# Low parts of the unscaled weights computed on GpSimd instead of VectorE, in a four-layer hybrid decoder

## The chip, the cores and the metric

One core of one Trainium2 chip runs the whole program. The metric is the device time of one execution in microseconds; the median of three runs counts. The engines are named as in the profile: PE is TensorE's matrix unit (PEld its weight load), DVE is VectorE, ACT is ScalarE, POOL is GpSimd, SP is SyncE, which issues most of the DMAs.

## What is computed

The reference is a decoder trunk of four layers over 1024 tokens of width 1024, batch 1, all in float32. Layers 0 and 3 mix tokens with an HGRN2 gated linear recurrence (8 heads), layer 1 with sliding-window attention (16 query heads, 4 key/value heads, window 128), layer 2 with a gated DeltaNet (8 query/key heads, 16 value heads, a short causal convolution ahead of it). Cut to the frame:

```python
for i in range(DEPTH):
    mod = (c @ ada_w[i] + ada_b[i])[:, None, :]
    shift, scale, gate = jnp.split(mod, 3, axis=-1)
    h = rmsnorm(x, norm_g[i]) * (1.0 + scale) + shift
    y = mixer[i % 3](h, ...)       # (o * silu(z)) @ w_out, with q, k, v, z from h @ w_in
    x = x + gate * y
return x
```

Most of the arithmetic is in `h @ w_in` and `... @ w_out`.

## The kernel before

**Numbers in two parts.** A projection is not multiplied in plain float32. Weights and activations are split into a high part (type `F32R` in the code) and a low part, the rest: `hi = cast(x)`, `lo = x - hi`. A product is then three matmuls, high by high, and each high by the other's low; `mm3` (L196 to L198) issues them. In the profile these are the groups `proj_ps` (feature-major, 128x512), `projt_ps` (token-major, 128x256) and `outp_ps` (output projection).

**A weight tile's way.** `load_w` (L158 to L178) brings 128x512 floats into a buffer `w_raw` (L169, an SP DMA of 256 KB; tag "raw", three buffers, shared with the modulation weights `ada_w`), makes `w_hi` on ACT and then `w_lo`. There are four buffers each of w_hi and w_lo. So w_raw comes free when w_lo has been made, and w_hi and w_lo when PE has used them. There are two forms. Without a scale (all input projections, and the window layer's output projection) w_hi is an ACT cast (L171) and w_lo a subtraction (L172), 332 of each. With a scale (the other output projections, which fold a norm's gain into the weights) it is L174 and L175, 136 of each.

**What else the engines do.** PE runs the projections and the small matmuls of the mixers. DVE has the elementwise work of the mixers, the normalisations (n_t at L479, then hlo at L481, which reads n_t and hhi), the modulation sums (L403, L405), the convolution taps (L617, L619) and, in the DeltaNet layer, a serial elimination on 32x32 blocks (L750, L751). GpSimd has little: copies of diagonal blocks in the HGRN layers (L1044, `hg_at`), in the DeltaNet layer the convolution's three-column halo (L614, L608), memsets (L606, L741 to L743) and copies of block inverses (L773, L774, L783).

**What sets the order.** The program is written as generators (`weave`) which interleave the recurrence of one head with the projections of the next. A planner then lists the instructions of each engine by priority and by the time at which it reckons each to be ready, so an instruction that changes its engine changes the lists of all engines. On the chip every engine works through its own list in order and waits at semaphores.

**Stages in the profiled execution.** Start to about 60 us; HGRN layer 0 to 580 (its output projection runs on beyond that); changeover into the window layer to 700, window layer to about 1130; changeover into the DeltaNet layer to 1300, its loop over head pairs to 1960, output projection to 2200; HGRN layer 3 to the end.

Of the kernel before, what the change touches and what calls it, by code (L numbers as in the profile page):

```python
# [10 lines left out]
F32 = mybir.dt.float32  # L11
# [5 lines left out]
ALU = mybir.AluOpType  # L17
# [67 lines left out]
class Trunk:  # L85
# [72 lines left out]
    def load_w(self, src, scale=None):  # L158

        nc = self.nc  # L160
        shape = list(src.shape)
        raw = self.wp.tile([P, HT], F32, name="w_raw", tag="raw", bufs=RAW)
        hi = self.wp.tile([P, HT], F32R, name="w_hi", tag="whi", bufs=WB)
        lo = self.wp.tile([P, HT], F32R, name="w_lo", tag="wlo", bufs=WB)
        raw, hi, lo = (x[:, :math.prod(shape[1:])] for x in (raw, hi, lo))
        if len(shape) == 3:
            raw, hi, lo = (x.rearrange("p (a b) -> p a b", a=shape[1]) for x in (raw, hi, lo))
        with self.tc.high_priority(offset=self.pw):
            nc.sync.dma_start(raw, src)  # L169
            if scale is None:  # L170
                nc.scalar.copy(hi, raw)  # L171
                nc.vector.tensor_tensor(lo, raw, hi.bitcast(F32), ALU.subtract)  # L172
            else:
                nc.scalar.activation(hi, raw, AF.Copy, scale=scale)  # L174
                nc.vector.scalar_tensor_tensor(lo, raw, scale, hi.bitcast(F32), ALU.mult, ALU.subtract)  # L175
            n = self.tc.cur_priority
        self.tc.cur_priority = n + self.pw
        return hi, lo  # L178
# [1269 lines left out]
```

## Time and profile before

| | |
|---|---|
| median of three runs | 2753.58 us (2751.43 to 2759.05) |
| the profiled execution | 2752.67 us, span 2751.0 us |
| PE busy | 2669.9 us (97%) |
| DVE busy | 2001.3 us (73%) |
| ACT busy | 1224.1 us (44%) |
| GpSimd busy | 133.8 us (5%) |
| L172 (w_lo without scale) | 332 instructions, 223.1 us on DVE |

A row of a group gives line, engine, operation, output and inputs, shapes and count, then busy time and mean length of one, then the idle time of the engine just ahead of the group and what ended most of it. A row of waits reads "who, line <- for whom, line: us in total, times, longest". A row by stage gives the stretch, its length and then, engine by engine, the busy time and the number of instructions; the last three figures are the granted clock of PE, the busy share of the DMA engines and their GB/s. Rows of the timeline and of the chain begin with the start and the duration in us.

### The profile page before, as it was taken

How to read it: one execution, taken by the hardware profiler on the slowest of the kernel's cores; microseconds unless marked ns; L12 is line 12 of the kernel's file. 1: busy time of each engine (PE TensorE's matmuls, PEld its weight loads, DVE VectorE, ACT ScalarE, POOL GpSimd, SP SyncE). 2: the span in 40 equal slices, each digit the busy share in tenths (PEclk: the TensorE clock that was granted, in tenths of full speed). 3: DMA queues.
4: the chain of work that ended last, by engine and by line, in shares of the span. 5: the costliest groups of instructions: out<-in, count | busy, mean ns of one | idle time of the engine just before them, and what ended most of it. 6: DMA issues, size and time to landing. Idle time of an engine off the chain costs nothing.

```text
span 2751.0 us, 51716 instructions
## 1 busy us (share of the span) xinstructions
PE 2669.9 (97%) x19217; PEld 2147.2 (78%) x19217; DVE 2001.3 (73%) x5669; ACT 1224.1 (44%) x3107; POOL 133.8 (5%) x352
## 2 busy tenths in 40 slices
PE   8999999998999999899999999999999999999999
PEld 4878888778878767677788877787778888887877
DVE  6685765778677778677898798988875757556575
ACT  4332333444445565444546455555543433333342
POOL 0000100000000000001101001100000000000000
PEclk9999999999999999999999999999999999999999
DMA  6232222344223243324343343432463211111133
GB/s 237 82 103 82 66 85 74 118 129 146 62 85 97 77 149 91 116 74 111 94 127 101 92 123 101 116 104 77 150 188 119 81 54 40 51 46 49 46 120 112
DMA packets 347666, 273.30 MB, mean 99 GB/s; under 512 B 68963, under 2 KB 276246, under 8 KB 347414
## 3 DMA queue, kind: packets, MB, share of 16 engines
q1 hardware_dynamic: 347126, 268.95, 32.8%
q8 instruction: 151, 2.47, 0.4%
q14 instruction: 101, 0.83, 0.1%
q0 software_dynamic: 288, 1.05, 0.1%
HBM read 224.77 MB, written 45.15 MB: 98 GB/s over the span
## 4 chain that ended last, share of the span: by engine, by line
PE 76%; DVE 11%; DMA 6%; ACT 4%; issue 2%; SPq 1%; POOL 0%; DVEq 0%; ACTq 0%
PE proj_ps L196 10%; PE proj_ps L198 10%; PE proj_ps L197 10%; PE outp_ps L198 4%; PE outp_ps L196 4%; PE outp_ps L197 4%; PE projt_ps L197 3%; PE projt_ps L198 3%; PE projt_ps L196 3%; DMA ada_w<-in_ada_w_dram 2%; PE lev_ps L1004 2%; DVE gd_tb L617 1%; PE pv_ps L1330 1%; DVE w_lo L172 1%; PE w_ps L859 1%
## 5 line engine op out<-in xcount | busy, mean ns | idle before, releaser
L196 PE MATMUL proj_ps<-hhi,w_hi 128*128 128x512 f32 x1664 | 686.1, 412 | 11.2 <-ACT gd_tb L615 8.6
L197 PE MATMUL proj_ps<-hlo,w_hi 128*128 128x512 f32 x1664 | 675.5, 406 | 0.0
L198 PE MATMUL proj_ps<-hhi,w_lo 128*128 128x512 f32 x1664 | 674.0, 405 | 0.0
L196 PEld LDWEIGHTS proj_ps<-hhi,w_hi 128*128 128x128 f32 x1664 | 315.5, 190 | 68.3 <-ACT gd_tb L615 11.0
L198 PEld LDWEIGHTS proj_ps<-hhi,w_lo 128*128 128x128 f32 x1664 | 314.9, 189 | 59.1 <-issue 1.2
L197 PEld LDWEIGHTS proj_ps<-hlo,w_hi 128*128 128x128 f32 x1664 | 315.3, 190 | 53.0 <-issue 1.4
L172 DVE TENSOR_TENSOR w_lo<-w_raw,w_hi 128x512 fp32r<-128x512 f32 x332 | 223.1, 675 | 168.2 <-ACT w_hi L171 165.6
L171 ACT CAST w_hi<-w_raw 128x512 fp32r<-128x512 f32 x332 | 201.9, 611 | 307.8 <-PE proj_ps L197 183.1
L197 PE MATMUL projt_ps<-w_lo,hhi 128*128 128x256 f32 x896 | 256.1, 290 | 5.8 <-DVE w_lo L172 5.8
L196 PE MATMUL projt_ps<-w_hi,hhi 128*128 128x256 f32 x896 | 256.1, 291 | 0.5 <-ACT w_hi L171 0.5
L198 PE MATMUL projt_ps<-w_hi,hlo 128*128 128x256 f32 x896 | 255.4, 290 | 0.0
L196 PE MATMUL outp_ps<-o_hi,w_hi 128*128 128x512 f32 x576 | 229.3, 400 | 2.9 <-ACT o_hi L1156 1.9
L198 PE MATMUL outp_ps<-o_hi,w_lo 128*128 128x512 f32 x576 | 228.0, 398 | 1.4 <-DVE w_lo L175 1.4
L197 PE MATMUL outp_ps<-o_lo,w_hi 128*128 128x512 f32 x576 | 228.8, 398 | 0.2
L197 PEld LDWEIGHTS projt_ps<-w_lo,hhi 128*128 128x128 f32 x896 | 170.7, 192 | 9.2 <-DVE w_lo L172 6.8
L196 PEld LDWEIGHTS projt_ps<-w_hi,hhi 128*128 128x128 f32 x896 | 170.5, 192 | 3.8 <-issue 1.2
L198 PEld LDWEIGHTS projt_ps<-w_hi,hlo 128*128 128x128 f32 x896 | 170.6, 192 | 2.3 <-issue 1.4
L617 DVE SCALAR_TENSOR_TENSOR gd_tb<-gd_xs,taps,gd_tb 128x512 f32<-128x512 f32 x192 | 144.2, 751 | 25.1 <-ACT gd_tb L615 21.5
L174 ACT ACTIVATE w_hi<-w_raw,par 128x512 fp32r<-128x512 f32 (+1 forms) x136 | 94.7, 698 | 142.9 <-PE outp_ps L197 98.8
L196 PEld LDWEIGHTS outp_ps<-o_hi,w_hi 128*128 128x128 f32 x576 | 108.6, 189 | 27.0 <-ACT o_hi L1156 3.9
L175 DVE SCALAR_TENSOR_TENSOR w_lo<-w_raw,par,w_hi 128x512 fp32r<-128x512 f32 (+1 forms) x136 | 96.8, 716 | 42.8 <-ACT w_hi L174 41.5
L198 PEld LDWEIGHTS outp_ps<-o_hi,w_lo 128*128 128x128 f32 x576 | 108.6, 189 | 24.2 <-DVE w_lo L175 1.9
(388 smaller groups left out, 4918.5 us busy)
## 6 DMA issues: line engine op xcount, KB each, us to landing
ada_w<-in_ada_w_dram SPq DMA_DIRECT2D x160, 256.0 KB, 2.8
w_raw<-in_hg_in_w_dram SPq DMA_DIRECT2D x136, 256.0 KB, 2.8
w_raw<-in_gd_in_w_dram SPq DMA_DIRECT2D x108, 256.0 KB, 3.1
o_in<-od SPq DMA_DIRECT2D x72, 256.0 KB, 3.3
w_raw<-in_gd_out_w_dram SPq DMA_DIRECT2D x64, 256.0 KB, 2.8
w_raw<-in_sw_in_w_dram SPq DMA_DIRECT2D x48, 256.0 KB, 3.0
w_raw<-in_hg_out_w_dram SPq DMA_DIRECT2D x40, 256.0 KB, 2.9
ada_w<-in_ada_w_dram SPq DMA_DIRECT2D x8, 1024.0 KB, 10.0
```

The costliest lines, as they stand in the source:

```text
L171: nc.scalar.copy(hi, raw)
L172: nc.vector.tensor_tensor(lo, raw, hi.bitcast(F32), ALU.subtract)
L174: nc.scalar.activation(hi, raw, AF.Copy, scale=scale)
L175: nc.vector.scalar_tensor_tensor(lo, raw, scale, hi.bitcast(F32), ALU.mult, ALU.subtract)
L196: mm(out, a[0], b[0], start=start, stop=False)
L197: mm(out, a[0], b[1], start=False, stop=False)
L198: mm(out, a[1], b[0], start=False, stop=stop)
L617: nc.vector.scalar_tensor_tensor(y, xs[:, j:j + HT], w(j), y, ALU.mult, ALU.add)
L859: nc.tensor.matmul(po[:, hd[a]], dd["u"][a, hf][:, cs], rhs, start=True, stop=True)
L1004: nc.tensor.matmul(pl[gs, c * 48:(c + 1) * 48], kg[:, c * P + g * 32:c * P + (g + 1) * 32], x[:, 4 * c + g, :], start=True, stop=True)
L1330: nc.tensor.matmul(po[a * 64:(a + 1) * 64], vg[:, n + 1 - nkb + b, :], p4[:, :, a, :], start=b == 0, stop=b == nkb - 1)
```

## The change

One line: where a weight tile has no scale, the subtraction that makes w_lo is issued on GpSimd.

```diff
             if scale is None:
                 nc.scalar.copy(hi, raw)
-                nc.vector.tensor_tensor(lo, raw, hi.bitcast(F32), ALU.subtract)
+                nc.gpsimd.tensor_tensor(lo, raw, hi.bitcast(F32), ALU.subtract)
```

The scaled form (L175) stays on VectorE, and so does every other low part. All 332 move, and the planner's order moves with them on every engine.

On VectorE, at the start of the DeltaNet layer, in the normalisation of the second half of the tokens (x_11272 is that half of x), the order of before has w_lo between the steps:

```order
L466 TENSOR_TENSOR n_sq<-ident,rs_y 128x512
L479 SCALAR_TENSOR_TENSOR n_t<-x_11272,gcol,n_rb 128x512 x2
L481 SCALAR_TENSOR_TENSOR hlo<-n_t,mod,hhi 128x512
L172 TENSOR_TENSOR w_lo<-w_raw,w_hi 128x512
L481 SCALAR_TENSOR_TENSOR hlo<-n_t,mod,hhi 128x512
L172 TENSOR_TENSOR w_lo<-w_raw,w_hi 128x512
L479 SCALAR_TENSOR_TENSOR n_t<-x_11272,gcol,n_rb 128x512 x2
L481 SCALAR_TENSOR_TENSOR hlo<-n_t,mod,hhi 128x512
```

The same place in the changed program, on the same engine:

```order
L466 TENSOR_TENSOR n_sq<-ident,rs_y 128x512
L479 SCALAR_TENSOR_TENSOR n_t<-x_11272,gcol,n_rb 128x512 x2
L481 SCALAR_TENSOR_TENSOR hlo<-n_t,mod,hhi 128x512 x2
L479 SCALAR_TENSOR_TENSOR n_t<-x_11272,gcol,n_rb 128x512 x2
L481 SCALAR_TENSOR_TENSOR hlo<-n_t,mod,hhi 128x512
L479 SCALAR_TENSOR_TENSOR n_t<-x_11272,gcol,n_rb 128x512
```

The five w_lo that stood among these sixteen steps (two are among the rows shown) have left VectorE's list.

On GpSimd, in the DeltaNet loop, where the first block inverse is put together (gd_Tb is the elimination's result of the next head pair, gd_Z and gd_uq hold the assembled inverse, gd_xs and gd_halo belong to the convolution), the order of before:

```order
L741 MEMSET gd_Tb 128x512
L742 MEMSET gd_Tb 64x16
L743 MEMSET gd_Tb 64x16
L773 COPY gd_Z<-gd_Tc 32x16x32
L774 COPY gd_Z<-gd_Tc 32x16x32
L783 COPY gd_uq<-gd_Uc 32x16x32 x4
L614 COPY gd_halo<-gd_xs 128x3
L608 COPY gd_xs<-gd_halo 128x3
```

And in the changed program:

```order
L741 MEMSET gd_Tb 128x512
L172 TENSOR_TENSOR w_lo<-w_raw,w_hi 128x512
L742 MEMSET gd_Tb 64x16
L743 MEMSET gd_Tb 64x16
L172 TENSOR_TENSOR w_lo<-w_raw,w_hi 128x512
L773 COPY gd_Z<-gd_Tc 32x16x32
L774 COPY gd_Z<-gd_Tc 32x16x32
L783 COPY gd_uq<-gd_Uc 32x16x32 x4
L172 TENSOR_TENSOR w_lo<-w_raw,w_hi 128x512 x6
L614 COPY gd_halo<-gd_xs 128x3
L608 COPY gd_xs<-gd_halo 128x3
```

Eight w_lo now stand among the copies, two ahead of those of the block inverse and six between them and the next halo.

## The prediction

> **What bounds the kernel now.** I read the page's busy table first, then the costliest groups, the busy time by stage, the waits, and last the timeline at the places where TensorE (PE) stood still.
>
> ```profile
> span 2751.0 us, 51716 instructions
> PE 2669.9 (97%) x19217; PEld 2147.2 (78%) x19217; DVE 2001.3 (73%) x5669; ACT 1224.1 (44%) x3107; POOL 133.8 (5%) x352
> ...
> L172 DVE TENSOR_TENSOR w_lo<-w_raw,w_hi 128x512 fp32r<-128x512 f32 x332 | 223.1, 675 | 168.2 <-ACT w_hi L171 165.6
> L171 ACT CAST w_hi<-w_raw 128x512 fp32r<-128x512 f32 x332 | 201.9, 611 | 307.8 <-PE proj_ps L197 183.1
> ```
>
> PE is busy for 2669.9 of 2751.0 us. The change takes no matmul away, so all it can win is part of the other 81 us and of short pauses that this busy figure hides. VectorE (DVE) works 73% of the time; GpSimd (POOL) is nearly free.
>
> By stage (columns: PE, PEld, DVE, ACT, POOL busy; PEclk is the granted clock), and below it the part of L172 alone in DVE's time:
>
> ```profile
> 60.00:580.00 520.00, 514.40 (x4550) 424.82 (x4550) 355.80 (x1082) 185.41 (x426) 31.37 (x65) 1.00 0.30 90
> 580.00:700.00 120.00, 108.12 (x672) 93.52 (x672) 94.87 (x220) 50.54 (x95) 1.58 (x4) 0.97 0.42 131
> 700.00:1000.00 300.00, 292.27 (x1951) 234.26 (x1949) 212.14 (x642) 149.16 (x389) 0.00 (x0) 1.00 0.29 90
> 1130.00:1300.00 170.00, 152.30 (x895) 117.51 (x895) 120.73 (x306) 79.05 (x220) 12.97 (x33) 0.96 0.34 91
> 1300.00:1960.00 660.00, 649.42 (x4542) 525.55 (x4541) 571.44 (x1673) 356.02 (x1110) 54.41 (x135) 0.99 0.39 107
> ```
>
> ```profile
> 60.00:580.00 520.00, 44.04 (x64) 1.00 0.30 90
> 1300.00:1960.00 660.00, 52.09 (x76) 0.99 0.39 107
> ```
>
> The long stages (HGRN 60 to 580, the DeltaNet loop 1300 to 1960) leave PE idle for 5.6 and 10.6 us. The changeovers into the window layer (580 to 700) and into the DeltaNet layer (1130 to 1300) leave 11.9 and 17.7 us, and there the granted clock dips as well. In the DeltaNet loop DVE is at 87%.
>
> **The change part by part.**
>
> *What leaves DVE.* 332 instructions of 675 ns. Back to back, a DVE instruction occupies less than its length:
>
> ```profile
> 1243.05 0.69 DVE L172 TENSOR_TENSOR w_lo<-w_raw,w_hi 128x512 fp32r<-128x512 f32 x1
> 1243.65 0.28 DVE L751 TENSOR_TENSOR gd_Tb<-gd_Tb,gd_tmp 128x126 f32<-128x126 f32 x1
> ```
>
> The next one starts 0.60 us later, so 332 x 0.60 = 199 us of DVE's queue go. With them go 165.6 us in which DVE's queue stood still until ACT had made w_hi. Most of both lies beside PE work. What shows on the path is in three waits of PE and the places behind them:
>
> ```profile
> PE proj_ps L196 <- ACT gd_tb L615: 8.6, 4, 5.9
> PE projt_ps L197 <- DVE w_lo L172: 5.8, 4, 2.9
> PE vtr_ps L625 <- DVE gd_tb L619: 5.7, 4, 3.7
> ```
>
> First, the window layer's opening. w_hi, w_lo and the matmul that wants it:
>
> ```profile
> 678.55 1.14 ACT L171 CAST w_hi<-w_raw 128x512 fp32r<-128x512 f32 x2
> 681.53 0.62 ACT L171 CAST w_hi<-w_raw 128x512 fp32r<-128x512 f32 x1 [1.19 <-DMA w_raw<-in_sw_in_w_dram]
> 684.52 0.69 DVE L172 TENSOR_TENSOR w_lo<-w_raw,w_hi 128x512 fp32r<-128x512 f32 x1
> 685.26 0.38 PE L197 MATMUL projt_ps<-w_lo,hhi 128*128 128x256 f32 x1 [0.52 <-DVE w_lo L172]
> 687.10 0.69 DVE L172 TENSOR_TENSOR w_lo<-w_raw,w_hi 128x512 fp32r<-128x512 f32 x1
> 687.85 0.39 PE L197 MATMUL projt_ps<-w_lo,hhi 128*128 128x256 f32 x1 [0.90 <-DVE w_lo L172]
> ```
>
> The two w_hi were ready at 679.7 and 682.2, but their w_lo stood in DVE's queue until 684.5 and 687.1. An idle GpSimd would deliver both by 683.5 even at 1.3 us each, so these two waits (0.52 + 0.90) go. The other two waits of the 5.8 us hang on a raw buffer and its load as well; I take a quarter of their 4.4 us, 1.1. Together 2.5 us.
>
> Second, the DeltaNet layer's opening, in the chain of waits:
>
> ```profile
> 1136.43 0.70 DVE w_lo L172
> 1137.15 2.83 DMA w_raw<-in_gd_in_w_dram
> ...
> 1140.73 0.69 DVE w_lo L172
> 1141.42 0.68 DVE hlo L481
> ...
> 1143.42 0.60 DVE w_lo L172
> 1144.02 1.33 DVE hlo L481 x2
> ```
>
> Between the normalisation's n_t and hlo, on which everything waits here, the order of before has five w_lo, that of the changed program none: 5 x 0.60 = 3.0 us off a chain behind which PE waited 5.9 us. But hlo reads two SBUF tiles, and the next paragraph shows that it will sometimes stand behind a w_lo on GpSimd; I take 2.0 us. The same squeeze stands ahead of the window layer and in the first DeltaNet weave (the 5.7 us at L625): together I take 2.0 more. Gain: 2.5 + 2.0 + 2.0 = 6.5 us.
>
> *What GpSimd now does.* No two-input operation of GpSimd is in the trace. Its nearest row is a one-input copy of 512 elements, beside DVE:
>
> ```profile
> L783 POOL COPY gd_uq<-gd_Uc x32: 599/786/1142, 1275.3 to 1958.7; 32x512 f32<-32x512 f32 x32
> ...
> 1358.70 3.66 POOL L783 COPY gd_uq<-gd_Uc 32x512 f32<-32x512 f32 x4
> ...
> 1358.71 1.14 DVE L619 SCALAR_TENSOR_TENSOR gd_q<-gd_tb 128x512 f32<-128x512 f32 x1
> 1360.15 1.73 DVE L722 TENSOR_TENSOR gd_tmp<-gd_tmp,gd_cmask 128x512 f32<-128x512 f32 x2
> ...
> L619 DVE SCALAR_TENSOR_TENSOR gd_k<-gd_tb 128x512 f32<-128x512 f32 x16 | 11.0, 690 | 4.0 <-ACT gd_tb L618 3.9
> ```
>
> Undisturbed it takes 599 ns. Two reads of 512 elements one after the other make 1.2 us: my value for w_lo, with 0.6 us as the lower end. 332 x 1.2 = 398 us, 14% of the span. The Trainium skill (GPSIMD Engine Reference, section 3.1) gives 4497 ns for a two-input add of 2048 elements; a quarter of that is an estimate of 1.12 us, by which the sum would be the same.
>
> *The two engines block each other.* In these rows L619 began 10 ns after GpSimd's copy and took 1.14 us in place of 0.69: it stood still 0.45 us. And GpSimd's copies stretch from 599 to 1142 ns. The worst case is a copy of three elements, otherwise about 0.19 us:
>
> ```profile
> 1243.06 2.54 POOL L608 COPY gd_xs<-gd_halo 128x3 f32<-128x3 f32 x1 [5.02 <-DVE gd_tb L617]
> ```
>
> DVE ran two-SBUF-input instructions without a gap and GpSimd got in only after 2.4 us. So a w_lo lasts 0.6 to some 3.6 us (1.2 + 2.4). The Trainium skill (SBUF — State Buffer, "Who interferes with whom") states it as a rule: a DVE instruction with two SBUF inputs and a GpSimd one that reads SBUF take turns, whole instructions at a time. This trace agrees (0.45 us of standing still beside a 0.6 us copy). By the rule to the letter a w_lo would cost a blocked instruction 1.2 us where I take 1.0 below, which changes DVE's sum by 10 us and PE's by nothing; how it could turn the result is the second rival.
>
> In the DeltaNet loop: 76 w_lo leave, 76 x 0.60 = 46 us. Most big DVE groups there have both inputs in SBUF; taking two in three, each blocked for 1.0 of the 1.2 us, 76 x 0.67 x 1.0 = 51 us come back. Net +5 us on an engine that has 89 us idle: nothing for PE. At 0.6 us a w_lo the same sum gives -23 us, at 2.5 us of blocking +81. In the HGRN stages DVE has a third of its time free, so I charge 2.5 us for all the blocking there, from 0 to 8.
>
> *Latency of w_lo.* From the release of a buffer it was 0.61 (ACT) + 0.69; now 0.61 + 1.2. PE spends 24 matmuls on a tile:
>
> ```profile
> 56.59 0.39 PE L198 MATMUL proj_ps<-hhi,w_lo 128*128 128x512 f32 x1
> 56.82 0.40 PE L196 MATMUL proj_ps<-hhi,w_hi 128*128 128x512 f32 x1
> ```
>
> 24 x 0.23 = 5.5 us, which hides 1.8. The token-major projections are tighter:
>
> ```profile
> 685.60 0.28 PE L196 MATMUL projt_ps<-w_hi,hhi 128*128 128x256 f32 x1
> 685.72 0.28 PE L197 MATMUL projt_ps<-w_lo,hhi 128*128 128x256 f32 x1
> ```
>
> Their first pass over 128 tokens takes 24 matmuls of 0.12 us, 2.9 us, and wants all four tiles of a block, the last one after 2.2 us. Against 1.8 us that leaves some 0.4 us where the last buffer comes free only as the block begins. There are about sixteen such blocks, mostly with other matmuls to run beside them: I charge 1 us, at most 16 x 0.4 = 6.
>
> *Queues.* GpSimd works in order. Behind a w_lo now stand the copies L1044, L608, L783 and behind their waits stands the next w_lo:
>
> ```profile
> POOL hg_at L1044 <- DVE hg_A L1039: 703.0, 24, 105.3
> ```
>
> These 703 us are idle time of an early-placed copy. The planner has put the w_lo that are due meanwhile ahead of it, so the wait is not inherited. ACT's and SP's instructions stay; the raw buffer comes free when w_lo ends, 0.5 us later on a free DVE, but earlier where DVE's queue was the delay. Both are in the sums above.
>
> *Sum.* -6.5 + 2.5 + 1.0 = -3.0 us. The profiled execution took 2752.7 us (span 2751.0); 2752.7 - 3.0 = 2749.7, and since it lies 0.9 us under the median of 2753.6, on the median's scale about 2750. I name 2750.
>
> **The rivals.** A measurement of this kernel tells some 0.3%, 8 us, from no change.
>
> *Faster (2738).* The planner's whole order moves with the change, and DVE was saturated before nearly every pause of PE. If relief wins in both changeovers and in the window layer, half of 11.9 + 17.7 and of 7.7 us goes, 18.7 us, less 3.5 of costs: -15, and 2752.7 - 15 + 0.9 = 2738. For it: the long waits of w_lo in DVE's queue. Against it: most of the DVE work at those places has two SBUF inputs.
>
> *Slower (2769).* The take-turns lock. If a w_lo costs DVE 2.5 us of blocking in the DeltaNet loop (as the L608 row would suggest once the longer operation holds the port), DVE's 571 - 46 + 127 = 652 of 660 us leave it no slack. If a fifth of the added 81 us reaches PE (my choice: today's blocking reaches it in less, but DVE has slack today), that is 16 us: 2752.7 + 16 + 0.9 = 2769, the gains at the openings being lost in the same way. It decides from a DVE share of 95% (627 us) in that loop. For it: the rows above. Against it: 0.45 us was all that one blocking cost there.
>
> *The change doing nothing at all* is not one: all 332 stand on GpSimd's queue in the new program. What stays on DVE are the 136 scaled ones at L175.
>
> **How the numbers follow.** Little change 0.38, faster 0.35, slower 0.27: the gains are seen in rows, the lock is seen as well, and neither is large against 8 us. The likeliest is 2750, its own range 2743 to 2758. Both rivals lie within reach, so the range runs from 2733 (the faster one and 5 us more) to 2773 (the slower one and 4).
>
> **What would show it.** Right: PE's waits at projt L197 for w_lo gone; no w_lo in the chain at the DeltaNet opening; w_lo on GpSimd near 1.2 us in HGRN and longer in the DeltaNet loop; DVE's busy time down by less than 223 us because its two-input instructions lengthened; PE within 3 us of 2670. Wrong: DVE's busy time in the DeltaNet loop above 627 us, PE waiting on DVE groups there (L617, L751), or w_lo of 2 us and more in the mean; or PE's idle time under 70 us.

## The result, and the profile after

| | before | after |
|---|---|---|
| median | 2752.97 us (2750.17 to 2760.59, 6 runs) | 2883.38 us (2871.89 to 2898.90, 6 runs) |
| ratio | | 1.0467, 95% interval 1.0447 to 1.0487 |

130 us slower, where 3 us faster was predicted; even the slower rival (2769) fell far short. The profiled execution of after took 2898.9 us, the longest of its six, so the account of its span (146 us above that of before) has some 15 us more in it than the medians have.

The page of after: span, busy time, and the group of L172, now on GpSimd:

```profile
span 2897.2 us, 51763 instructions
...
PE 2728.3 (94%) x19217; PEld 2181.4 (75%) x19217; DVE 1948.3 (67%) x5337; ACT 1224.1 (42%) x3107; POOL 569.2 (20%) x684
...
L172 POOL TENSOR_TENSOR w_lo<-w_raw,w_hi 128x512 fp32r<-128x512 f32 x332 | 442.4, 1339 | 1516.2 <-ACT w_hi L171 1266.5
```

332 instructions with 223 us of busy time left DVE, and its busy time fell by only 53 (2001.3 to 1948.3): what stayed became longer. PE's idle time went from 81 to 169 us, and PE itself was busy 58 us longer with the same 19217 matmuls.

The mean granted clock of TensorE, before and after:

```profile
core 0: 2751.0 us, clock 0.993
```

```profile
core 0: 2897.2 us, clock 0.977
```

(1 - 0.993) x 2751 = 19 us and (1 - 0.977) x 2897 = 67 us: 47 of the 58 us are, by this estimate, a lower clock. So the 146 us of the spans are 88 us in which PE stood still, 47 us of clock and some 11 us of the rest. The share of the clock is that of this one execution: the six of after have a mean clock of 0.977 to 0.987, and 0.977 is the lowest.

What PE waits for now (waits of after: us in total, times, longest):

```profile
PE vtr_ps L625 <- DVE gd_tb L619: 16.4, 17, 2.3
PE pt_ps L1324 <- DVE sw_sm L1318: 12.3, 15, 1.9
PE ot_ps L1099 <- DVE hg_tmp L1095: 10.6, 17, 3.7
PE w_ps L859 <- DVE gd_wg L861: 8.2, 10, 1.4
```

These four, the largest, are all for work of DVE, in every kind of layer: many short waits, not one bottleneck. Added up over all rows of the view, PE waited 124 us for DVE (42 before), 20 for ACT (21 before) and 7 for GpSimd (none before): nearly all of the 88 us more are waits that DVE ended. Yet no stage has a full DVE (after by stage; columns as in the prediction):

```profile
60.00:580.00 520.00, 497.06 (x4454) 408.93 (x4454) 317.63 (x995) 175.82 (x412) 111.62 (x128) 0.99 0.28 85
1360.00:2060.00 700.00, 657.84 (x4311) 526.82 (x4309) 563.58 (x1556) 345.66 (x1078) 154.18 (x202) 0.96 0.34 94
```

In the first HGRN layer DVE is busy 61% of the time, and PE is idle for 23 us where it was 5.6; in the DeltaNet loop DVE is at 81%, less than before, and PE is idle for 42 us.

One of the waits from close by: the first head of HGRN, where four numbers per partition go through L1092 and the inverse root (L151 to L155) on DVE, then L1095, for which PE's ot_ps stands. First before, in the timeline:

```profile
141.72 0.16 DVE L1092 TENSOR_SCALAR hg_ms<-hg_ssq 128x4 f32<-128x4 f32 x1
141.92 0.17 DVE L151 TENSOR_SCALAR rs_y<-hg_ms 128x4 int32<-128x4 int32 x1
...
145.83 0.69 DVE L1095 TENSOR_TENSOR hg_tmp<-o_ps,rs_y 128x512 f32<-128x512 f32 x1
...
146.67 0.30 PE L1099 MATMUL ot_ps<-ident,hg_tmp 128*128 128x128 f32 x1 [0.79 <-DVE hg_tmp L1095]
```

And after, the same steps:

```profile
145.49 0.62 ACT L171 CAST w_hi<-w_raw 128x512 fp32r<-128x512 f32 x1 [2.01 <-DMA w_raw<-in_hg_in_w_dram]
146.01 0.27 ACT L1090 ACTIVATE hg_tmp<-o_ps 128x128 f32<-128x128 f32 x1
146.19 2.54 POOL L172 TENSOR_TENSOR w_lo<-w_raw,w_hi 128x512 fp32r<-128x512 f32 x2 [17.95 <-ACT w_hi L171]
146.41 1.09 DVE L1092 TENSOR_SCALAR hg_ms<-hg_ssq 128x4 f32<-128x4 f32 x1 [2.96 <-ACT hg_tmp L1090]
147.53 1.22 DVE L151 TENSOR_SCALAR rs_y<-hg_ms 128x4 int32<-128x4 int32 x1
...
151.69 0.68 DVE L1095 TENSOR_TENSOR hg_tmp<-o_ps,rs_y 128x512 f32<-128x512 f32 x1
...
152.52 0.45 PE L1099 MATMUL ot_ps<-ident,hg_tmp 128*128 128x128 f32 x1 [3.70 <-DVE hg_tmp L1095]
```

Two w_lo run on GpSimd without a gap, 2.54 us. L1092, of four elements, begins beside the first and ends with it (1.09 us in place of 0.16); L151 begins beside the second and ends with it (1.22 in place of 0.17). Nothing else ran on DVE meanwhile: it was not full, it was held up. Ahead of it stands a second delay. ACT works in order, and L1090, which the chain waits for, stood behind a w_hi that waited 2.01 us for its w_raw. Together they make a wait of 3.70 us for PE where there was one of 0.79.

The Trainium skill (SBUF — State Buffer, "Who interferes with whom") counts among the DVE instructions that GpSimd blocks not only those with two SBUF inputs but also single-input ones in a two-port mode, tensor_scalar among them; the prediction used only the first half. The 1.09 us of L1092, a TENSOR_SCALAR with one tensor input, agree with the second.

### The profile page after: what moved, and what is told of

It is laid out like the page before. It is cut to its first block, busy times and chain, and to the rows that moved or that the text cites. A ratio compares the mean times of both kernels' runs of the same rounds, so it can differ in the third digit from the quotient of the medians.

```text
span 2897.2 us, 51763 instructions
## 1 busy us (share of the span) xinstructions
PE 2728.3 (94%) x19217; PEld 2181.4 (75%) x19217; DVE 1948.3 (67%) x5337; ACT 1224.1 (42%) x3107; POOL 569.2 (20%) x684
## 5 line engine op out<-in xcount | busy, mean ns | idle before, releaser
L172 POOL TENSOR_TENSOR w_lo<-w_raw,w_hi 128x512 fp32r<-128x512 f32 x332 | 442.4, 1339 | 1516.2 <-ACT w_hi L171 1266.5
L198 PE MATMUL proj_ps<-hhi,w_lo 128*128 128x512 f32 x1664 | 681.7, 410 | 2.9 <-POOL w_lo L172 2.9
L197 PE MATMUL proj_ps<-hlo,w_hi 128*128 128x512 f32 x1664 | 683.3, 411 | 0.0
L198 PEld LDWEIGHTS proj_ps<-hhi,w_lo 128*128 128x128 f32 x1664 | 318.8, 192 | 61.7 <-POOL w_lo L172 4.2
L197 PEld LDWEIGHTS proj_ps<-hlo,w_hi 128*128 128x128 f32 x1664 | 319.1, 192 | 56.5 <-issue 3.3
L197 PE MATMUL projt_ps<-w_lo,hhi 128*128 128x256 f32 x896 | 255.7, 291 | 4.5 <-POOL w_lo L172 4.5
L198 PE MATMUL projt_ps<-w_hi,hlo 128*128 128x256 f32 x896 | 254.5, 289 | 0.0
L198 PE MATMUL outp_ps<-o_hi,w_lo 128*128 128x512 f32 x576 | 228.1, 397 | 1.1 <-DVE w_lo L175 1.0
L197 PE MATMUL outp_ps<-o_lo,w_hi 128*128 128x512 f32 x576 | 228.6, 398 | 0.2
L617 DVE SCALAR_TENSOR_TENSOR gd_tb<-gd_xs,taps,gd_tb 128x512 f32<-128x512 f32 x192 | 164.3, 856 | 36.2 <-ACT gd_tb L615 31.2
L197 PEld LDWEIGHTS projt_ps<-w_lo,hhi 128*128 128x128 f32 x896 | 171.2, 193 | 9.4 <-POOL w_lo L172 6.3
L198 PEld LDWEIGHTS projt_ps<-w_hi,hlo 128*128 128x128 f32 x896 | 171.1, 193 | 1.3 <-issue 0.8
L405 DVE SCALAR_TENSOR_TENSOR ada_acc<-ada_w,par,ada_acc 128x512 f32<-128x512 f32 x140 | 105.7, 755 | 52.3 <-DMA ada_w<-in_ada_w_dram 51.0
L175 DVE SCALAR_TENSOR_TENSOR w_lo<-w_raw,par,w_hi 128x512 fp32r<-128x512 f32 (+1 forms) x136 | 96.8, 716 | 43.8 <-ACT w_hi L174 41.2
```

Of the source, the lines that this page charges most:

```text
L172: nc.gpsimd.tensor_tensor(lo, raw, hi.bitcast(F32), ALU.subtract)
L197: mm(out, a[0], b[1], start=False, stop=False)
L198: mm(out, a[1], b[0], start=False, stop=stop)
L405: self.nc.vector.scalar_tensor_tensor(acc, w, c, acc, ALU.mult, ALU.add)
L617: nc.vector.scalar_tensor_tensor(y, xs[:, j:j + HT], w(j), y, ALU.mult, ALU.add)
```

## The experiments

Three explanations stood against each other. **A**: a two-input w_lo on GpSimd and DVE take turns, and DVE's chains come late. **B**: the planner's new order is worse by itself. **C**: w_lo is ready later and the raw buffer is free later. Differences are to the runs of before on the same chip.

### The blocking alone: a pair of twins

The kernel before keeps w_lo on DVE; GpSimd gets an additional instruction whose result nobody reads. The first twin subtracts, the second only writes. Their instructions stand in the same order on PE, DVE, ACT and SP.

```diff
                 nc.vector.tensor_tensor(lo, raw, hi.bitcast(F32), ALU.subtract)
+                nc.gpsimd.tensor_tensor(raw, raw, hi.bitcast(F32), ALU.subtract)   # first twin
+                nc.gpsimd.memset(raw, 0.0)                                         # second twin
```

> The kernel before, with w_lo still made by VectorE; GpSimd runs the same subtraction a second time, into the raw buffer that nobody reads any more. No matmul waits for GpSimd. Theory A (GpSimd reading two SBUF tiles and VectorE take turns, and VectorE's short chains arrive late): VectorE keeps its 223 us of w_lo and still gets the lengthening of about 137 us, so at least as slow as the changed kernel, 2870 us or more. Theory B (the changed order of the instructions is what is worse): as fast as its twin with the write (same order on TensorE, VectorE, ScalarE and SyncE), within 8 us. Theory C (raw buffers come free later): slower than before, 2780 to 2830, and the twin with the write is slower too, by about 0.5/1.3 of that.

> The twin: the same program, but GpSimd fills the raw buffer with zeros where the other one subtracts. It writes 128x512 and reads nothing (such a fill takes 0.52 us in the trace of before). TensorE, VectorE, ScalarE and SyncE have exactly the order of the first twin. Theory A: no lengthening of VectorE's instructions, 2745 to 2765 us. Theory B: whatever the first twin takes, within 8 us. Theory C: slower than before by some 10 to 35 us.

First twin: 2886.13 us, ratio 1.0465 (1.0437 to 1.0492), +132.5 us. Second: 2762.99 us, 1.0031 (1.0014 to 1.0049), +9.4 us. First twin, the page, then from the groups on DVE:

```profile
span 2884.4 us, 52415 instructions
...
PE 2715.2 (94%) x19217; PEld 2166.2 (75%) x19217; DVE 2137.9 (74%) x5669; ACT 1224.5 (42%) x3107; POOL 593.2 (21%) x684
```

```profile
L617 DVE SCALAR_TENSOR_TENSOR gd_tb<-gd_xs,taps,gd_tb 128x512 f32<-128x512 f32 x192 | 156.4, 814 | 24.3 <-ACT gd_tb L615 19.3 <-issue 3.0 <-POOL gd_halo L614 1.1
L751 DVE TENSOR_TENSOR gd_Tb<-gd_Tb,gd_tmp 128x126 f32<-128x126 f32 (+22 forms) x248 | 74.8, 302 | 3.1
...
L1102 DVE TENSOR_TENSOR hg_tmp<-ot_ps,hg_zs 128x512 f32<-128x512 f32 x32 | 22.0, 687 | 2.0 <-PE ot_ps L1099 1.5
```

Second twin, the same views:

```profile
span 2760.9 us, 52379 instructions
...
PE 2678.7 (97%) x19217; PEld 2150.4 (78%) x19217; DVE 2004.7 (73%) x5669; ACT 1223.8 (44%) x3107; POOL 304.0 (11%) x684
```

```profile
L617 DVE SCALAR_TENSOR_TENSOR gd_tb<-gd_xs,taps,gd_tb 128x512 f32<-128x512 f32 x192 | 144.8, 754 | 26.2 <-ACT gd_tb L615 22.2 <-issue 3.0
L751 DVE TENSOR_TENSOR gd_Tb<-gd_Tb,gd_tmp 128x126 f32<-128x126 f32 (+22 forms) x248 | 62.5, 252 | 3.1
...
L1102 DVE TENSOR_TENSOR hg_tmp<-ot_ps,hg_zs 128x512 f32<-128x512 f32 x32 | 22.0, 689 | 1.5 <-PE ot_ps L1099 0.7
```

The same 5669 DVE instructions take 133.2 us longer (2137.9 against 2004.7) when GpSimd reads as well as writes. L617 and L751, with their inputs in SBUF, lengthen; L1102, one of whose inputs lies in PSUM, does not (687 and 689 ns). The order can't be the cause, it is the same: B falls for the bulk of the loss, and A holds. PE's idle time grows by 87 us (82.2 to 169.2), and its waits for DVE by 79 (43 to 122).

A fill is not wholly without effect. In the second twin the L151 of the example above began beside one and ended with it, 0.55 us in place of 0.17:

```profile
143.18 0.53 POOL L172 MEMSET w_raw<- 128x512 f32 x1 [17.20 <-DVE hg_ms L1092]
143.18 0.55 DVE L151 TENSOR_SCALAR rs_y<-hg_ms 128x4 int32<-128x4 int32 x1
```

In all it is little: DVE's 2004.7 us are 3.4 above those of before.

The twins differ in one more thing: the subtraction holds the raw buffer longer. So a third version fills it three times, 1.56 us:

```diff
+                [nc.gpsimd.memset(raw, 0.0) for _ in range(3)]
```

> The twin with the write, with GpSimd filling the raw buffer three times (3 x 0.52 = 1.56 us), so that it is held about as long as by the subtraction (1.3 us undisturbed) and ScalarE's next load comes as late, but GpSimd reads nothing. Theory A (the taking of turns carries the loss): within 25 us of the kernel before, 2755 to 2780. Theory C (the raw buffers coming free late carries it): 2830 us or more. Whatever it takes above the kernel before is the part of the first twin's 133 us that the blocking did not cause.

2781.81 us, 1.0091 (1.0063 to 1.0119), +24.8 us. Its order is different on every engine, so I read it as a size: about 25 of the 132 us belong to C, some 108 to the blocking. The third version does not hold the buffer too short: GpSimd ends with it 1.75 us after DVE's w_lo in the median, 1.43 in the first twin and 0.63 in the second.

### The changed kernel without the reading

GpSimd fills w_lo with zeros at once, so that the subtraction, and with it the low part of these products, is left out:

```diff
-                nc.gpsimd.tensor_tensor(lo, raw, hi.bitcast(F32), ALU.subtract)
+                nc.gpsimd.memset(lo.bitcast(F32), 0.0)
```

> The changed kernel with the subtraction left out: GpSimd fills w_lo with zeros, reading nothing. VectorE is relieved of all 332 w_lo, the planner makes a new order again. Theory A: at or below the kernel before, 2735 to 2755 us, VectorE's L617 back at about 750 ns in the mean. Theory B (a new order of this kind costs by itself): still 2830 us or more. Theory C: w_lo is ready early and the raw buffers come free early, so also below 2755; it is told from A by the twins.

2725.64 us, 0.9893 (0.9866 to 0.9920): 28.0 us faster than before, a little better than A expected. The page:

```profile
span 2725.1 us, 51642 instructions
...
PE 2662.8 (98%) x19217; PEld 2140.4 (79%) x19217; DVE 1816.3 (67%) x5337; ACT 1223.7 (45%) x3107; POOL 296.1 (11%) x684
```

So 28 us are gained with 185 us less of DVE's time (2001.3 to 1816.3). The relief of DVE is not all of it: the fill waits for neither w_raw nor w_hi, so w_lo is ready earlier here than in the kernel before, and w_raw comes free as soon as w_hi is made. The changed kernel has the same DVE instructions, and they take 132.0 us more there.

The same, meant to have w_lo as late as in the changed kernel (GpSimd copies one column of w_hi, fills twice, copies one column of w_raw; the subtraction is left out here too):

```diff
+                nc.gpsimd.tensor_copy(fl(lo)[:, 0:1], fl(hi)[:, 0:1])
+                nc.gpsimd.memset(fl(lo)[:, 1:-1].bitcast(F32), 0.0)      # twice
+                nc.gpsimd.tensor_copy(fl(lo)[:, -1:], fl(raw)[:, -1:])
```

> The changed kernel with the subtraction left out, but with its lateness kept: GpSimd waits for w_hi, copies one column of it, fills the tile with zeros twice and copies one column of the raw buffer at the end, so w_lo is ready and the raw buffer free about 1.4 us after w_hi (0.2 + 0.52 + 0.52 + 0.2 from rows of such instructions), with hardly any reading. Theory A (only the taking of turns costs): within 10 us of the kernel that only fills w_lo, 2725 to 2740. Theory C (lateness of w_lo and of the raw buffers is a good part): 2755 to 2800.

2748.49 us, 0.9964 (0.9947 to 0.9982), -7.9 us. It lies between the two expectations: the lateness that it has costs about 20 us (28.0 - 7.9) against w_lo filled at once, more than A allowed and less than C wanted. The page's busy line has DVE at 1821.4 us, so there was next to no blocking in it:

```profile
PE 2677.0 (97%) x19217; PEld 2144.9 (78%) x19217; DVE 1821.4 (66%) x5337; ACT 1222.8 (44%) x3107; POOL 556.4 (20%) x1680
```

But the run does not keep the whole lateness. The program was planned in another order: for most tiles one fill runs before w_hi is there, and the copy of w_raw before the last fill. One tile in the timeline, whose w_hi ended at 302.58:

```profile
302.17 0.53 POOL L172 MEMSET w_lo<- 128x510 f32 x1 [8.29 <-PE proj_ps L198]
302.65 0.18 POOL L172 CAST w_lo<-w_hi 128x1 fp32r<-128x1 f32 x1
```

The copy that frees w_raw ends 0.37 us after w_hi in the median; in the changed kernel the subtraction ends 1.38 us after it. So the 20 us are no measure of the changed kernel's lateness, nor are they counted from the kernel before, where w_lo ended 0.84 us after w_hi in the median and 1.97 in the mean (1.59 in the changed kernel). What the lateness costs there stays open but for one thing: PE waited for w_lo itself 7.4 us, and 5.8 before.

### One input in place of two

GpSimd copies w_hi into w_lo (the subtraction is left out):

```diff
+                nc.gpsimd.tensor_copy(lo, hi)
```

> The changed kernel, but GpSimd copies w_hi into w_lo: one input in place of two, the subtraction left out; GpSimd's copy of 512 elements took 0.6 us in the trace of before. If a GpSimd instruction with one SBUF input holds VectorE up too, for its length: the loss against the kernel that only fills w_lo (2725.6) is 0.6/1.29 of the changed kernel's 158 us, so about 2799 us (2780 to 2815). If only two-input GpSimd instructions do: about 2726 us.

2754.68 us, 0.9996 (0.9980 to 1.0013): neither number. Its page:

```profile
PE 2676.8 (97%) x19217; PEld 2144.9 (78%) x19217; DVE 1849.0 (67%) x5337; ACT 1223.2 (44%) x3107; POOL 349.0 (13%) x684
...
L172 POOL CAST w_lo<-w_hi 128x512 fp32r<-128x512 f32 x332 | 223.7, 675 | 1613.1 <-ACT w_hi L171 1372.5
```

224 us of copies lengthen DVE by 33 us (1849.0 against 1816.3), 0.15 us for each us of GpSimd; 442 us of subtractions lengthen it by 132, 0.30 for each us. The blocking grows faster than the time that GpSimd is busy. Why is not settled by this run.

### Where it is lost

w_lo on GpSimd in one kind of layer only:

```diff
-                nc.gpsimd.tensor_tensor(lo, raw, hi.bitcast(F32), ALU.subtract)
+                (nc.gpsimd if self.cur == 2 else nc.vector).tensor_tensor(lo, raw, hi.bitcast(F32), ALU.subtract)
```

(self.cur is the layer whose body is being written; `self.cur % 3 == 0` for the HGRN layers.)

> w_lo on GpSimd only in the DeltaNet layer (and the loads that its body makes), on VectorE elsewhere. By the places of the same loads in the two profiles, the DeltaNet layer is where 83 of the 146 us between the two profiled executions were lost. Theory A: the loss sits where VectorE is fullest, so 2753 + 83 (75 to 90) = about 2836 us, and the other layers have their length of before. Theory B: the order elsewhere is nearly the old one, the order in this layer is new: also a loss, but VectorE's instructions keep their length. Theory C: 2753 + 20 to 40.

> w_lo on GpSimd only in the two HGRN layers (where VectorE has a third of its time free), on VectorE in the window and the DeltaNet layer. The DeltaNet layer alone lost 63 us, all together 130; by the places of the same loads in the two profiles HGRN lost 36 and the window layer 26 of the remaining 62. Theory A with the losses adding up by layer: 2753 + 38 = about 2791 us (2780 to 2803). My prediction's term of 2.5 us for blocking where VectorE has time to spare: 2756 (2750 to 2762).

DeltaNet alone: 2816.64 us, 1.0229 (1.0190 to 1.0268), +63.0. HGRN alone: 2793.53 us, 1.0131 (1.0109 to 1.0152), +37.6. Where the layers begin can be read from the first matmuls of the keys in the window layer (L1237) and in the DeltaNet layer (ktr_ps, L625), and the end of the loop from the last of L859. The rows end with the first and last start; before:

```profile
L1237 PE MATMUL kt_ps<-ident,sw_tmp x32: 271/272/273, 650.0 to 692.1; 128*64 128x128 f32 x32
L625 PE MATMUL ktr_ps<-ident,gd_k x64: 271/273/333, 1152.8 to 1851.9; 128*128 128x128 f32 x64
L859 PE MATMUL w_ps<-gd_y,gd_uq x224: 270/275/421, 1293.9 to 2031.5; 128*128 128x128 f32 x112
```

and after:

```profile
L1237 PE MATMUL kt_ps<-ident,sw_tmp x32: 270/272/421, 671.2 to 722.7; 128*64 128x128 f32 x32
L625 PE MATMUL ktr_ps<-ident,gd_k x64: 271/273/474, 1204.2 to 1966.7; 128*128 128x128 f32 x64
L859 PE MATMUL w_ps<-gd_y,gd_uq x224: 270/275/580, 1360.0 to 2162.2; 128*128 128x128 f32 x112
```

The stretches between these times, against before, in us, of the profiled executions:

| w_lo on GpSimd | first HGRN (650.0) | window (502.8) | DeltaNet (878.7) | the rest, HGRN (719.5) |
|---|---|---|---|---|
| everywhere (after) | +21.2 | +30.2 | +79.3 | +15.5 |
| DeltaNet only | +2.6 | +2.4 | +53.0 | +0.5 |
| HGRN only | +18.8 | +2.8 | +3.3 | +15.8 |

The HGRN and the DeltaNet layers lose where their own w_lo moved; the window layer's were never moved alone. The HGRN layers lose as much by themselves as in the whole, 34.6 against 36.7 us; the DeltaNet layer loses 26 us less by itself. Some 15 us of the first row are the length of that one execution above its median; the rest is open. The busy lines of the two pages, DeltaNet only and then HGRN only:

```profile
PE 2687.1 (96%) x19217; PEld 2154.2 (77%) x19217; DVE 2012.4 (72%) x5561; ACT 1224.4 (44%) x3107; POOL 280.6 (10%) x460
...
L172 DVE TENSOR_TENSOR w_lo<-w_raw,w_hi 128x512 fp32r<-128x512 f32 x224 | 149.0, 668 | 158.7 <-ACT w_hi L171 157.1
```

```profile
PE 2685.9 (96%) x19217; PEld 2158.8 (77%) x19217; DVE 1948.6 (70%) x5533; ACT 1222.6 (44%) x3107; POOL 311.6 (11%) x488
...
L172 DVE TENSOR_TENSOR w_lo<-w_raw,w_hi 128x512 fp32r<-128x512 f32 x196 | 129.6, 664 | 30.5 <-ACT w_hi L171 28.1
```

From these the lengthening: 2012.4 - (2001.3 - 223.1 + 149.0) = 85 us for the DeltaNet layer's 108 w_lo, 0.79 us each; 1948.6 - (2001.3 - 223.1 + 129.6) = 41 us for the 136 of HGRN, 0.30 each.

### The openings alone

Only the 28 tiles that are loaded ahead at the openings go to GpSimd, the place of the predicted gain (four of them at the first layer's):

```diff
+                (nc.gpsimd if self.pw else nc.vector).tensor_tensor(lo, raw, hi.bitcast(F32), ALU.subtract)
```

> w_lo on GpSimd only for the 28 tiles that are loaded ahead at the openings of the window, the DeltaNet and the last layer, where the prediction saw w_lo standing in VectorE's queue and put down a gain of 6.5 us. If that gain is real apart from the blocking elsewhere: 2747 us, 2744 to 2750, faster than before. If the blocking takes it back even there (28 tiles at 0.4 us): 2754 to 2765.

2768.80 us, 1.0042 (1.0027 to 1.0056), +12.9 us, beyond even the pessimistic expectation: 0.46 us a tile. The page, and then the two groups of the normalisation on DVE:

```profile
PE 2676.7 (97%) x19217; PEld 2152.9 (78%) x19217; DVE 1992.7 (72%) x5641; ACT 1222.0 (44%) x3107; POOL 173.3 (6%) x380
...
L172 DVE TENSOR_TENSOR w_lo<-w_raw,w_hi 128x512 fp32r<-128x512 f32 (+1 forms) x304 | 204.2, 674 | 165.9 <-ACT w_hi L171 161.9
```

```profile
L481 DVE SCALAR_TENSOR_TENSOR hlo<-n_t,mod,hhi 128x512 fp32r<-128x512 f32 x64 | 48.9, 791 | 4.1 <-ACT hhi L480 2.7 <-DMA w_raw<-in_hg_in_w_dram 0.2
L458 DVE TENSOR_TENSOR n_acc<-n_acc,n_sq 128x512 f32<-128x512 f32 x42 | 32.5, 774 | 3.2 <-ACT n_sq L457 1.5
```

Without the moved w_lo, DVE should have 2001.3 - 223.1 + 204.2 = 1982.4 us; it has 1992.7, 10 us of blocking. Much of it sits in the normalisation on which everything waits at an opening: hlo has a mean of 791 ns (746 before) and n_acc 774 (688 before).

The two longest waits of the opening among PE's stayed:

```profile
PE vtr_ps L625 <- DVE gd_tb L619: 6.9, 5, 3.7
PE proj_ps L196 <- ACT gd_tb L615: 6.8, 4, 4.5
```

13.7 us together, 14.3 before (5.7 and 8.6, rows of the prediction). PE's waits for w_lo did shrink, from 5.8 to 2.6 us (1.6 for DVE, 1.0 for GpSimd), and its other waits for DVE grew by some 10.

### Shorter pieces

Each w_lo on GpSimd in four instructions of a quarter of the columns:

```diff
+                for q in range(4):
+                    nc.gpsimd.tensor_tensor(fl(lo)[:, q * n4:(q + 1) * n4], fl(raw)[:, q * n4:(q + 1) * n4],
+                                            fl(hi)[:, q * n4:(q + 1) * n4].bitcast(F32), ALU.subtract)
```

> The changed kernel with each w_lo made by GpSimd in four instructions of a quarter of the columns. From the 725 and 1260 ns of undisturbed 256- and 512-column ones I work out some 0.46 us for 128 columns, so GpSimd's time grows by a third. Theory A1 (VectorE loses what GpSimd holds in all, however it is cut, since the two alternate): 2870 to 2930 us, VectorE's busy time not below the changed kernel's 1948. Theory A2 (what hurts is how long a single blocking lasts): 2790 to 2840 us, blocked small VectorE instructions at 0.6 us in place of 1.3.

2872.20 us, 1.0424 (1.0394 to 1.0455), +116.3. A2 is out. A1 has its time right but its reason wrong: DVE's busy time did fall below 1948.

```profile
PE 2719.2 (95%) x19217; PEld 2170.0 (76%) x19217; DVE 1896.7 (66%) x5337; ACT 1224.2 (43%) x3107; POOL 766.3 (27%) x1680
```

To see whether the rest was w_lo's lateness, the same cut was made in the first twin, where nobody waits for GpSimd:

> The kernel before with the unused second subtraction on GpSimd cut into four instructions of a quarter of the columns. No matmul waits for it. In the changed kernel the same cut brought VectorE's lengthening from 132 down to 80 us and the time down by only 11. If blocking passes on at its length and the rest of that kernel's loss is the lateness of w_lo: 2753 + 9 + 80 = 2842 us (2825 to 2855). If the taking of turns costs what GpSimd holds in all, however it shows: 2875 us or more.

2914.34 us, 1.0559 (1.0515 to 1.0603), +158.0. DVE's busy time:

```profile
PE 2705.2 (94%) x19217; PEld 2158.4 (75%) x19217; DVE 2090.6 (72%) x5669; ACT 1223.2 (42%) x3107; POOL 809.8 (28%) x1680
```

It is 86 us above the second twin, and yet the kernel is slower than with whole subtractions. So cutting shortens what can be seen in DVE's lengths and gives no time back: PE still waits 127 us for DVE (122 with whole subtractions), and 40 for ACT (28). Where the other 70 us go is open; one part is seen in the waits, ACT standing for its weights' DMA longer (for the HGRN input weights alone 61.5 us, 37.8 in the first twin), since GpSimd lets the raw buffers go later (2.30 us after DVE's w_lo in the median, 1.43 there).

### The same amount on DVE, in its place

The kernel before, with DVE repeating five eighths of each subtraction, and nothing for GpSimd:

```diff
+                nc.vector.tensor_tensor(fl(raw)[:, :n5], fl(raw)[:, :n5], fl(hi)[:, :n5].bitcast(F32), ALU.subtract)
```

> The kernel before, with about as much work added to VectorE as the blocking added to it (133 us): after each w_lo it subtracts w_hi from five eighths of the raw buffer once more, 332 instructions of some 0.3 to 0.47 us, 128 us in all; GpSimd gets nothing new. Theory D (any microsecond more on VectorE costs about one microsecond here): 2870 us or more. Theory E (work that the planner knows of and that stands where it put it costs little; blocking in lumps of up to 1.3 us in the middle of a chain costs nearly its length): by the 28 us that the 223 us of w_lo are worth, 2753 + 128 x 28/223 = 2770 us (2760 to 2790).

2781.63 us, 1.0088 (1.0054 to 1.0121), +25.3 us, as E expected.

```profile
PE 2690.6 (97%) x19217; PEld 2165.4 (78%) x19217; DVE 2120.1 (76%) x6001; ACT 1224.4 (44%) x3107; POOL 133.0 (5%) x352
```

DVE carries 119 us more (2120.1 against 2001.3), nearly what the blocking put on it. Planned work costs 25 / 119 = 0.21 us per microsecond, and taking it away brought 28 / 185 = 0.15 at most, since the earlier w_lo is in the 28. The twins' blocking costs 108 / 133 = 0.8. The prediction made no such difference. Whether it is the planning that makes the added work cheap, or its place beside w_lo and off the short chains, this run does not tell. And 0.8 is no constant: cut into quarters, 86 us of lengthening went with 158 us of time.

## Why the prediction was wrong, point by point

The medians, put together from the runs: without GpSimd's reading, and with part of its lateness, -8 us (2748.49); with it +130. What lies between, 138 us, has 127 us of longer DVE time behind it (1948.3 against 1821.4) and, in a share that is not measured, the rest of the lateness. The twins and the third version put the blocking alone, in the kernel before, at some 108 us.

- **"Net +5 us on an engine that has 89 us idle: nothing for PE."** This step failed. The DeltaNet layer lost 53 us by itself in the profiled execution (63 in the median), and in the changed kernel DVE is at 81% of the loop. The amount of blocking was nearly right: 0.67 us a tile predicted, 0.79 measured. Wrong was to set it off against DVE's idle time. That idle time lies where DVE has nothing to do. The blocking falls on instructions in short chains behind which PE stands, as at 146 us, and idle time later does not give it back: PE's waits for DVE rose from 42 to 124 us.
- **"2.5 us for all the blocking there, from 0 to 8"** (HGRN). The same error: 35 to 38 us with a DVE busy 61% of the time. The example at 146 us shows how, two four-element instructions held for 2.1 us.
- **"-6.5 us at the openings."** Not found: +12.9 us with only those tiles moved. The w_lo did stand in DVE's queue, and PE's waits for them did fall, but moved to GpSimd they hold up the normalisation beside them, which is the opening's chain. Where nothing is blocked the whole kernel gains, 8 to 28 us by how early w_lo comes.
- **"1 us, at most 6" for latency.** Not refuted: PE's waits for w_lo, which were to go at L197, went from 5.8 to 7.4 us (4.5 at L197, 2.9 at L198), so they cost 1.6 us more. The sum left out ACT, which stands in order for the next w_raw with other work behind it, as in the example at 146 us; PE's waits that ACT itself ended did not grow (21 us before, 20 after), and what such delays add to DVE's chains is not measured.
- **The slower rival** had the right mechanism and the wrong condition. It "decides from a DVE share of 95%", and "a fifth" of the added time was to reach PE. DVE never came near 95% in the stages shown, and in the twins four fifths of the blocking showed in the time.
- **Not in the sum at all**: the clock. In the profiled execution 88 us more of PE's standing still came with 47 us of lower granted clock. The ratio is not fixed: with the work added to DVE, PE stood still for only 11 us more than before and the lower clock (0.985) cost some 22. What lowers it is not shown.
- **Right**: w_lo at 1.2 us (the median was 1.29; the Trainium skill's GPSIMD Engine Reference, section 3.1, gave an estimate of 1.12), a little longer in the mean where DVE is denser (1.38 us in the DeltaNet layer, 1.34 in HGRN); DVE's busy time falling by less than 223 us; and GpSimd's long waits not being inherited (703 us ahead of L1044 before, 165 after). PE's idle time was watched on the wrong side only: "under 70 us" was to be the sign of an error, and it rose to 169.
- **The chances**: slower had 0.27, and the range's 2773 rested on that fifth, which was chosen, not measured.

No version with w_lo on GpSimd that computes the reference beat the kernel before; the only faster ones left the subtraction out.

## What to carry to other kernels

An instruction that moves to an idle engine is not free if the two engines take turns at SBUF: price it by how long it holds up the other engine's chains, not by that engine's idle time. Work that the planner placed cost some 0.2 us per microsecond on DVE here, blocking by whole subtractions some 0.8. A cheap way to find out before moving anything: add the instruction unused on the other engine, once reading and once only writing, and compare the two.

## What the runs showed of the hardware

- A GpSimd subtraction of two 128x512 tiles in SBUF takes 1.29 us in the median; a copy 0.62, a fill 0.53. The fill, which reads nothing, left the lengths of two-input DVE instructions as they were (L617 754 and 751 ns) but held a TENSOR_SCALAR of four elements (L151 0.55 us in place of 0.17); the subtraction beside it made the same L617 814 to 856 ns in the mean.
- L1102, a DVE instruction with one of its two inputs in PSUM, was not lengthened: 687 ns in the mean with GpSimd's reading, 689 without. L1092, with one tensor input of four elements, was (0.16 to 1.09 us).
- Cutting GpSimd's reading into quarters made DVE's lengths shorter (1948.3 to 1896.7 us) and the kernel hardly faster (2883 to 2872 us).
